# An issue edge in the feed-forward part: the low half of a weight split moves behind a relu product

## The chip, the cores and the metric

The kernel runs on one core of one Trainium2 chip. The metric is the device time of one execution in microseconds (us). TensorE is PE in the rows (PEld its weight loads), VectorE is DVE, ScalarE is ACT, GpSimd is POOL, and SP is the engine that issues most transfers.

## The reference

One layer of a decoder block on a sequence of 1024 with width 1024. The change touches only its last two lines, the feed-forward part.

```
h = h + mixed @ w_out
hidden = jnp.square(jax.nn.relu(rmsnorm(h, norm2_gain) @ w_ff_in))   # 1024 x 4096
return h + hidden @ w_ff_out
```

## The kernel before

The feed-forward part works on one eighth of the 4096 hidden channels at a time: 8 pairs, each of an "up" phase (a piece of `w_ff_in`) and a "down" phase (a piece of `w_ff_out`), 16 phases in all. Each phase multiplies 2x2 blocks by Strassen's scheme in seven products, P1, P5, P6, P2, P7, P3, P4 in an up phase and P1, P5, P6, P3, P7, P2, P4 in a down phase. I call each product a step. Each product is made of float32r matmuls of a high and a low part: `hi*hi + hi*lo + lo*hi`, so that a step is 24 matmuls of 128x512 (`group`). In a row the tile that is named last is the one in the weights' place (`whi`, `wlo`) and the other one is streamed.

Around each step the other engines make operands for steps to come:

- `split_w` makes a step's weights: ACT casts the block to `whi`, DVE subtracts to get `wlo` (L936, L937). It is called one step ahead, under a raised priority. `whi` and `wlo` have two buffers each.
- After an up step the block of hidden values is finished in place: DVE adds the PSUM result (L1069), `act2` multiplies the relu with the norm's factors `r2` on DVE (L1001), and ACT squares (L1004). For P4 the relu reads PSUM directly (L1065) and so frees the PSUM bank `y0`. The blocks are c11 (from P2), c22 (P7), c12 (P3) and c21 (P4). In most rows their numbers are left out, so that all are `c`.
- `rhs` makes a down step's right-hand side: for P5, P6, P7 and P4 a difference of two blocks on DVE (`less`, L1021), then a cast to `thi` on ACT (L1031) and a subtraction to `tlo` on DVE (L1032). P5 of the down phase takes c12 - c11, P6 takes c22 - (c12 - c11), P7 takes c22 - c12.
- After each half of a down step DVE adds the PSUM result to `h` (L1094).
- POOL makes sums and differences of weight blocks in place (L967, L968, L970 and others). In a down phase L968 overwrites the block that P1's `wlo` reads and L970 overwrites `wa`, which P5's `wlo` reads; each therefore waits for that subtraction.

A scheduler, led by priorities and by when it expects an operand, puts the instructions of each engine in one fixed order; each engine then runs its list in that order. The down phase's P1 and P6 go to the PSUM banks `x0`, `x1`, P5 and P3 to `y0`, `y1`, so that P5 of the down phase writes into the bank that P4 of the up phase filled.

Of the kernel before, what the change touches and what calls it, by code (L numbers as in the profile page):

```python
# [11 lines left out]
F32 = mybir.dt.float32  # L12
# [3 lines left out]
ALU = mybir.AluOpType  # L16
# [4 lines left out]
P = 128  # L21
# [3 lines left out]
HALF = 512  # L25
# [34 lines left out]
def hybrid_block(ctx, tc, x_ap, xt_ap, win_ap, lora_ap, wbr_ap, wout_ap, wff1_ap, wff2_ap, cst_ap,  # L60
                 vec_ap, eye_ap, amk_ap, out_ap, dbg=None):
    nc = tc.nc
    V, A, G, PE = nc.vector, nc.scalar, nc.gpsimd, nc.tensor
# [43 lines left out]
    def vs_(name):  # L107
# [10 lines left out]
                    op1=ALU.add)  # L118
# [29 lines left out]
    def w_tile(dt, tag):  # L148
        return wpool.tile([P, NK, 128], dt, tag=tag, name=tag, bufs=2)

    def load_w(src, nk=NK, eng=None):
        raw, hi, lo = w_tile(F32, "wraw"), w_tile(F32R, "whi"), w_tile(F32R, "wlo")
        for k in range(0, nk, 4):
            ks = slice(k, k + 4)
            nc.sync.dma_start(out=raw[:, ks], in_=src[:, ks])
            A.copy(out=hi[:, ks], in_=raw[:, ks])  # L156
            (eng or V).tensor_sub(out=lo[:, ks], in0=raw[:, ks], in1=hi[:, ks].bitcast(F32))  # L157
        return [(hi[:, k], lo[:, k]) for k in range(nk)]
# [622 lines left out]
    for ct in range(NK):  # L781
        w = load_w(wbr_ap[ct])
        for hf in range(2):
# [12 lines left out]
                                   op0=ALU.mult, op1=ALU.subtract)  # L796
# [10 lines left out]
    def fetch(ph, name, t):  # L807
        nc.sync.dma_start(out=t, in_=(wff1_ap, wff2_ap)[ph % 2][ph // 2, idx[name]])
        return t
# [60 lines left out]
    def norm2(op, pz):  # L870
        pk = pz[:, 0, 0:16].rearrange("p (a b) -> p a b", b=2)
        pkf = pk.rearrange("p a b -> p (a b)")
        for hf in range(2):
            head_sums(pkf, 8 * hf, hs[hf])
        sm = op.tile([P, 8], F32, tag="sm", name="sm")
        V.tensor_reduce(out=sm, in_=pk, axis=AX.X, op=ALU.add)
        return newton(op, sm, 8, 1.0 / D, RMS_EPS)
# [17 lines left out]
    def res_sq(ct, hf):  # L895
        sl = slice(hf * HALF, (hf + 1) * HALF)
        if ct == 0:
            A.activation(out=hs[hf], in_=h[ct][:, sl], func=AF.Square)
        else:
            t = op.tile([P, HALF], F32, tag="tC", name="hq", bufs=2)  # L900
            A.activation(out=t, in_=h[ct][:, sl], func=AF.Square)
            V.tensor_add(out=hs[hf], in0=hs[hf], in1=t)

    def wout(ct):
        nc.sync.dma_start(out=h[ct], in_=xt_ap[ct * P:(ct + 1) * P, :])
        return load_w(wout_ap[ct])

    for ct in (0, 4, 1, 5, 2, 6):
        w = wout(ct)
# [11 lines left out]
    tags = (("m", 2), ("m", 2), ("s", 2), ("s", 2))  # L921
    pss = [(pm if t == "m" else pp).tile([P, HALF], F32, tag=t, name="ps_o", bufs=n) for t, n in tags]
    for k in range(NK):
        for j in range(4):
            w, sl = ws_[j // 2][k], slice((j % 2) * HALF, (j % 2 + 1) * HALF)
# [4 lines left out]
    gst = ExitStack()  # L930
    hp = gst.enter_context(tc.tile_pool(name="hpool", bufs=1, side="right"))

    def split_w(src, pool=None, tags=("whi", "wlo")):
        hi, lo = (w_tile(F32R, t) if pool is None else pool.tile([P, NK, 128], F32R, tag=t, name=t) for t in tags)
        with tc.high_priority(offset=HP_F):
            A.copy(out=hi, in_=src)  # L936
            V.tensor_sub(out=lo, in0=src, in1=hi.bitcast(F32))  # L937
        return hi, lo

    w0 = split_w(raw["a11"], hp, ("c21", "c22"))  # L940
    s1 = hp.tile([P, NK, 128], F32, tag="c12", name="s1")
    V.tensor_add(out=s1, in0=raw["a21"], in1=raw["a22"])  # L942
# [9 lines left out]
    r2 = mpool.tile([P, T], F32, tag="m14", name="r2")  # L952
    wa = mpool.tile([P, NK, 128], F32, tag="m15", name="wa")
    lo_, hi_ = slice(0, HALF), slice(HALF, T)
    hp2 = None
    nxt = {}

    def weight(ph, name):
        def ahead(new, old):
            if ph < 15:  # L960
                nxt[new] = fetch(ph + 1, new, raw[old])

        a11, a21, a12, a22 = (raw[k] for k in ("a11", "a21", "a12", "a22"))
        sm = wa if ph else s1
        w = w0 if ph == 0 and name == "P1" else split_w({"P1": a11, "P5": sm, "P6": a11, "P2": a12, "P7": a21, "P3": wa, "P4": a22}[name])
        if name == ("P5", "P1")[ph % 2]:
            G.tensor_sub(out=a21, in0=a11, in1=a21)  # L967
            G.tensor_sub(out=a11, in0=sm, in1=a11)  # L968
        elif name == "P6":
            (G if ph else V).tensor_sub(out=wa, in0=a12, in1=a11)  # L970
            ahead("a21", "a11")
        elif ph % 2 == 0:
            if name == "P2":
                ahead("a22", "a12")
            elif name == "P7":
                ahead("a11", "a21")
            elif name == "P3":
                G.tensor_add(out=wa, in0=nxt["a21"], in1=nxt["a22"])
            elif name == "P4":
                ahead("a12", "a22")  # L980
        else:
            if name == "P7":
                ahead("a11", "a21")
            elif name == "P2":
                ahead("a12", "a12")
            elif name == "P4":
                ahead("a22", "a22")
                if ph < 15:
                    G.tensor_add(out=wa, in0=nxt["a21"], in1=nxt["a22"])
        return w  # L990
# [6 lines left out]
                n += 1  # L997

    def act2(c, hf):
        if hf is not None:  # L1000
            V.scalar_tensor_tensor(out=c, in0=c, scalar=0.0,  # L1001
                                   in1=r2[:, (lo_, hi_)[hf]].unsqueeze(1).broadcast_to([P, 2, HALF]),
                                   op0=ALU.max, op1=ALU.mult)
        A.activation(out=c, in_=c, func=AF.Square)  # L1004

    rhs1 = {"P1": "B11", "P5": "T1", "P6": "T2", "P2": "B21", "P7": "T3", "P3": "B22", "P4": "T4"}
    dst1 = {"P1": "c11", "P5": "c22", "P6": "c12", "P2": "c11", "P7": "c22", "P3": "c12", "P4": "c21"}
# [5 lines left out]
    def bank(tag):  # L1013
        return (pf if tag[0] == "y" else px).tile([P, 2, HALF], F32, tag=tag, name="ps" + tag)
# [4 lines left out]
    def rhs(name):  # L1019
        def less(out, a):  # L1020
            V.tensor_sub(out=C[out], in0=C[a], in1=C[out])  # L1021

        if name == "P7":
            less("c12", "c22")
        with tc.high_priority(offset=HP_F if name in ("P5", "P6") else 0):
            if name in ("P5", "P6", "P4"):
                less("c11", {"P5": "c12", "P6": "c22", "P4": "c21"}[name])
            src = C[{"P3": "c22", "P7": "c12", "P2": "c21"}.get(name, "c11")]
            hi = hp2.tile([P, 2, HALF], F32R, tag="thi", name="thi", bufs=2)
            lo = hp2.tile([P, 2, HALF], F32R, tag="tlo", name="tlo", bufs=2)  # L1030
            A.copy(out=hi, in_=src)  # L1031
            V.tensor_sub(out=lo, in0=src, in1=hi.bitcast(F32))  # L1032
        R[name] = (hi, lo)

    def up(n, name, w):
        if name == "P1":
            for b in ("y0", "y1", "x0")[:2 if n == 0 else 3]:
                Z[b] = bank(b)
        if n == 0:
            if name not in ("P1", "P5"):  # L1040
                next(more, None)
            if name == "P6":
                for ct in (3, 7):
                    for hf in range(2):
                        res_sq(ct, hf)
                Z["rs"] = norm2(op, px1)
            if name == "P4":
                rhs("P1")
                rhs("P5")
        ps = Z[{"P5": "y1", "P3": "y1", "P2": "x0"}.get(name, "y0")]  # L1050
        hi, lo = w
        for a in range(2):
            group(ps[:, a], [((hi[:, 4 * a + k], lo[:, 4 * a + k]), B[rhs1[name]][k]) for k in range(4)],
                  name in ("P1", "P5", "P2"))
        cn = dst1[name]
        if name in ("P1", "P5", "P6", "P4"):
            C[cn] = hp.tile([P, 2, HALF], F32, tag=cn, name=cn)
        c = C[cn]
        if n == 0 and name == "P2":
            for hf in range(2):  # L1060
                spread(hf, Z["rs"], px1)
        if name in ("P1", "P5", "P6"):
            A.copy(out=c, in_=ps)
        elif name == "P4":
            V.scalar_tensor_tensor(out=c, in0=ps, scalar=0.0, in1=r2[:, lo_].unsqueeze(1).broadcast_to([P, 2, HALF]),  # L1065
                                   op0=ALU.max, op1=ALU.mult)
            act2(c, None)
        else:
            V.tensor_add(out=c, in0=c, in1=ps)  # L1069
            act2(c, 0 if name == "P2" else 1)  # L1070
            if hp2 is not None and name != "P7":
                rhs({"P2": "P1", "P3": "P5"}[name])

# [24 lines left out]

    steps = [(ph, name) for ph in range(16) for name in order[ph % 2]]
    w = weight(0, "P1")  # L1100
    for g, (ph, name) in enumerate(steps):
        nw = None
        if g + 1 < len(steps):
            if steps[g + 1][1] == "P1":
                raw, nxt = nxt, {}
# [6 lines left out]
        w = nw  # L1112
# [98 lines left out]
```

## Time and profile before

| what | before |
|---|---|
| median of 3 runs | 1527.97 us (1526.92 to 1528.69) |
| profiled execution | 1529.62 us, its span 1527.8 us |
| PE busy | 1491.3 us, 98% of the span |
| DVE busy | 1044.1 us, 68% |
| ACT busy | 639.1 us, 42% |
| POOL busy | 192.2 us, 13% |

The span runs from the first to the last recorded instruction. A busy share is an average over stages that differ: the feed-forward matmuls begin at 882 us of the span and go on to its end, and within each pair the load of DVE swings from nearly idle to unbroken.

### The profile page before, as it was taken

How to read it: one execution, taken by the hardware profiler on the slowest of the kernel's cores; microseconds unless marked ns; L12 is line 12 of the kernel's file. 1: busy time of each engine (PE TensorE's matmuls, PEld its weight loads, DVE VectorE, ACT ScalarE, POOL GpSimd, SP SyncE). 2: the span in 40 equal slices, each digit the busy share in tenths (PEclk: the TensorE clock that was granted, in tenths of full speed). 3: DMA queues.
4: the chain of work that ended last, by engine and by line, in shares of the span. 5: the costliest groups of instructions: out<-in, count | busy, mean ns of one | idle time of the engine just before them, and what ended most of it. 6: DMA issues, size and time to landing. Idle time of an engine off the chain costs nothing.

```text
span 1527.8 us, 22206 instructions
## 1 busy us (share of the span) xinstructions
PE 1491.3 (98%) x8396; PEld 1177.2 (77%) x8396; DVE 1044.1 (68%) x2056; ACT 639.1 (42%) x1126; POOL 192.2 (13%) x116
## 2 busy tenths in 40 slices
PE   5999999999999999999999999999999999999998
PEld 5878777777777777788888787878787878787776
DVE  4232678888988875353656579595858687776867
ACT  6332436456545665441224354332424333423332
POOL 1000000000000000000000111323223232323230
PEclk9999999999999999999999999999999999999999
DMA  5455334334222323383433111111120111111112
GB/s 192 165 149 146 109 103 149 103 104 120 88 90 66 103 84 124 117 295 113 136 125 146 42 42 56 56 42 69 42 69 28 69 42 65 46 56 42 56 55 111
DMA packets 99771, 145.65 MB, mean 95 GB/s; under 512 B 26448, under 2 KB 48848, under 8 KB 99664
## 3 DMA queue, kind: packets, MB, share of 16 engines
q1 hardware_dynamic: 99664, 144.23, 28.8%
q8 instruction: 66, 1.08, 0.3%
q14 instruction: 41, 0.34, 0.1%
HBM read 108.54 MB, written 35.65 MB: 94 GB/s over the span
## 4 chain that ended last, share of the span: by engine, by line
PE 75%; DVE 19%; ACT 3%; issue 2%; DMA 1%; SPq 0%; DVEq 0%; ACTq 0%
PE ps_m L164 32%; PE psy L996 15%; PE psx L996 12%; DVE wlo L937 4%; DVE c L1021 2%; DVE c L1001 2%; DVE tlo L1032 2%; PE po L164 2%; PE ps_o L927 1%; PE pu L170 1%; DVE h L1094 1%; ACT c L1004 1%; ACT whi L936 1%; PE pk L246 1%; PE ps_s L170 1%
## 5 line engine op out<-in xcount | busy, mean ns | idle before, releaser
L164 PE MATMUL ps_m<-uh,wlo 128*128 128x512 f32 x576 | 235.5, 409 | 0.0
L164 PE MATMUL ps_m<-ul,whi 128*128 128x512 f32 x576 | 234.3, 407 | 0.0
L164 PE MATMUL ps_m<-uh,whi 128*128 128x512 f32 x576 | 233.0, 404 | 0.0
L996 PE MATMUL psy<-T,whi 128*128 128x512 f32 x512 | 159.6, 393 | 0.0
L164 PEld LDWEIGHTS ps_m<-uh,whi 128*128 128x128 f32 x576 | 108.6, 189 | 21.2 <-issue 0.8
L164 PEld LDWEIGHTS ps_m<-uh,wlo 128*128 128x128 f32 x576 | 108.6, 189 | 21.1 <-issue 0.6
L164 PEld LDWEIGHTS ps_m<-ul,whi 128*128 128x128 f32 x576 | 108.7, 189 | 20.2 <-issue 0.7
L996 PEld LDWEIGHTS psy<-T,whi 128*128 128x128 f32 x512 | 96.1, 188 | 21.9
L157 DVE TENSOR_TENSOR wlo<-wraw,whi 128x512 fp32r<-128x512 f32 x101 | 67.9, 687 | 56.6 <-ACT whi L156 56.4
L996 PE MATMUL psx<-tlo,whi 128*128 128x512 f32 x256 | 101.9, 398 | 4.5 <-DVE tlo L1032 4.5
L937 DVE TENSOR_TENSOR wlo<-fraw_a,whi 128x1024 fp32r<-128x1024 f32 x47 | 66.0, 1405 | 57.5 <-ACT whi L936 57.5
L936 ACT CAST whi<-fraw_a 128x1024 fp32r<-128x1024 f32 x47 | 49.3, 1049 | 129.1 <-PE psy L996 85.7
L996 PE MATMUL psx<-thi,wlo 128*128 128x512 f32 x256 | 101.6, 398 | 1.5 <-DVE h L1094 0.9
L996 PE MATMUL psx<-thi,whi 128*128 128x512 f32 x256 | 101.0, 395 | 0.0
L996 PE MATMUL psy<-T,wlo 128*128 128x512 f32 x256 | 100.6, 393 | 0.0
L967 POOL TENSOR_TENSOR fraw_a<-fraw_a,fraw_a 128x1024 f32<-128x1024 f32 x16 | 45.5, 2846 | 346.7 <-DVE s L942 345.5
L1094 DVE TENSOR_TENSOR h<-h,psx 128x1024 f32<-128x1024 f32 (+1 forms) x66 | 76.8, 1179 | 9.6 <-PE psx L996 9.6
L996 PE MATMUL psy<-tlo,whi 128*128 128x512 f32 x192 | 77.2, 402 | 3.1 <-DVE tlo L1032 3.1
L156 ACT CAST whi<-wraw 128x512 fp32r<-128x512 f32 x105 | 61.0, 619 | 45.4 <-PE ps_m L164 45.3
L996 PE MATMUL psy<-thi,wlo 128*128 128x512 f32 x192 | 75.8, 395 | 0.0
L996 PE MATMUL psy<-thi,whi 128*128 128x512 f32 x192 | 75.8, 395 | 0.0
L996 PE MATMUL psy<-B,whi 128*128 128x512 f32 x240 | 74.8, 393 | 0.0
(298 smaller groups left out, 3227.1 us busy)
## 6 DMA issues: line engine op xcount, KB each, us to landing
wraw<-win SPq DMA_DIRECT2D x72, 256.0 KB, 3.3
fraw_a<-wff SPq DMA_DIRECT2D x32, 512.0 KB, 3.2
wraw<-wff SPq DMA_DIRECT2D x32, 512.0 KB, 3.2
gate_d<-gt SPq DMA_DIRECT2D x32, 256.0 KB, 2.0
z_d<-zt SPq DMA_DIRECT2D x24, 256.0 KB, 2.3
xt<-x SPq DMA_DIRECT2D x8, 512.0 KB, 5.7
la<-wa_d SPq DMA_DIRECT2D x8, 512.0 KB, 4.3
aq<-q_d SPq DMA_DIRECT2D x8, 512.0 KB, 4.2
```

The source lines that it names most:

```text
L156: A.copy(out=hi[:, ks], in_=raw[:, ks])
L157: (eng or V).tensor_sub(out=lo[:, ks], in0=raw[:, ks], in1=hi[:, ks].bitcast(F32))
L164: PE.matmul(out=out, lhsT=a, rhs=b, start=(n == 0), stop=(n == last))
L170: after = PE.matmul(out=out, lhsT=lhsT, rhs=rhs, start=start, stop=stop).ins
L936: A.copy(out=hi, in_=src)
L937: V.tensor_sub(out=lo, in0=src, in1=hi.bitcast(F32))
L967: G.tensor_sub(out=a21, in0=a11, in1=a21)
L996: PE.matmul(out=out, lhsT=a, rhs=b, start=start and n == 0, stop=n == last, skip_group_check=True)
L1001: V.scalar_tensor_tensor(out=c, in0=c, scalar=0.0, in1=r2[:, (lo_, hi_)[hf]].unsqueeze(1).broadcast_to([P, 2, HALF]), op0=ALU.max, op1=ALU ...
L1021: V.tensor_sub(out=C[out], in0=C[a], in1=C[out])
L1032: V.tensor_sub(out=lo, in0=src, in1=hi.bitcast(F32))
L1094: V.tensor_add(out=ht, in0=ht, in1=ps[:, c0 % 2:c0 % 2 + step])
```

## The change

The relu product of c12 (made in up step P3) is remembered, and the subtraction that makes `wlo` for P1 of the following down phase gets an issue edge on DVE: it stands behind that relu in DVE's list. An issue edge orders two instructions in one engine's list; it adds no wait. The number of instructions is the same on each engine, and PE's order is the same.

```diff
-    def split_w(src, pool=None, tags=("whi", "wlo")):
+    def split_w(src, pool=None, tags=("whi", "wlo"), after=None):
...
             A.copy(out=hi, in_=src)
-            V.tensor_sub(out=lo, in0=src, in1=hi.bitcast(F32))
+            with tc.issue_after(after) if after is not None else nullcontext():
+                V.tensor_sub(out=lo, in0=src, in1=hi.bitcast(F32))
...
+        w = w0 if ph == 0 and name == "P1" else split_w({"P1": a11, "P5": sm, "P6": a11, "P2": a12, "P7": a21, "P3": wa, "P4": a22}[name],
+                                                       after=relu.get((ph, name)))
...
-            act2(c, 0 if name == "P2" else 1)
+            last = act2(c, 0 if name == "P2" else 1)
+            if name == "P3":
+                relu[2 * n + 1, "P1"] = last
```

The scheduler then lays out DVE's list anew around the edge. This is DVE in the second pair before, from the addition for c12 to the addition of P1's second half to `h` (`wlo_10083` is P1's, `wlo_10116` and `tlo_10079` are P5's, all of the down phase):

```order
L1069 TENSOR_TENSOR c12_9975<-c12_9975,psy1_9886 128x1024
L937 TENSOR_TENSOR wlo_10083<-fraw_a21_8902,whi_10082 128x1024
L1001 SCALAR_TENSOR_TENSOR c12_9975<-c12_9975,r2_9323 128x1024
L1021 TENSOR_TENSOR c11_9912<-c12_9975,c11_9912 128x1024
L1065 SCALAR_TENSOR_TENSOR c21_10112<-psy0_9885,r2_9323 128x1024
L937 TENSOR_TENSOR wlo_10116<-wa_9324,whi_10115 128x1024
L1032 TENSOR_TENSOR tlo_10079<-c11_9912,thi_10078 128x1024
L1094 TENSOR_TENSOR h_8664<-h_8664,psx0_10119 128x2x512
L1021 TENSOR_TENSOR c11_9912<-c22_9944,c11_9912 128x1024
L1094 TENSOR_TENSOR h_8664<-h_8664,psx1_10120 128x2x512
```

And this is the same place of DVE's list in the changed kernel:

```order
L1073 TENSOR_TENSOR c12_9975<-c12_9975,psy1_9886 128x1024
L1004 SCALAR_TENSOR_TENSOR c12_9975<-c12_9975,r2_9323 128x1024
L938 TENSOR_TENSOR wlo_10083<-fraw_a21_8902,whi_10082 128x1024
L1025 TENSOR_TENSOR c11_9912<-c12_9975,c11_9912 128x1024
L1025 TENSOR_TENSOR c12_9975<-c22_9944,c12_9975 128x1024
L1036 TENSOR_TENSOR tlo_10079<-c11_9912,thi_10078 128x1024
L938 TENSOR_TENSOR wlo_10116<-wa_9324,whi_10115 128x1024
L1025 TENSOR_TENSOR c11_9912<-c22_9944,c11_9912 128x1024
L1069 SCALAR_TENSOR_TENSOR c21_10112<-psy0_9885,r2_9323 128x1024
L1100 TENSOR_TENSOR h_8664<-h_8664,psx0_10119 128x2x512
L1100 TENSOR_TENSOR h_8664<-h_8664,psx1_10120 128x2x512
```

Besides the swap of `wlo` and c12's relu, the difference for P7 (c12 - stored into c12) came up from behind P6's operands, the difference for P6 stands ahead of the additions to `h`, and the relu of c21 went from fifth place to ninth, behind all three differences and P5's two subtractions.

On ACT two casts changed places in each pair. Before, at the same place (`whi_10115` and `thi_10078` are P5's):

```order
L1004 ACTIVATE c12_9975<-c12_9975 128x1024
L936 CAST whi_10115<-wa_9324 128x1024
L1031 CAST thi_10078<-c11_9912 128x1024
L1004 ACTIVATE c21_10112<-c21_10112 128x1024
L936 CAST whi_10147<-fraw_a21_8902 128x1024
```

In the changed kernel:

```order
L1007 ACTIVATE c12_9975<-c12_9975 128x1024
L1035 CAST thi_10078<-c11_9912 128x1024
L936 CAST whi_10115<-wa_9324 128x1024
L1007 ACTIVATE c21_10112<-c21_10112 128x1024
L936 CAST whi_10147<-fraw_a21_8902 128x1024
```

P5's streamed operand now comes ahead of P5's weights. The rest of ACT's list is unmoved. All 8 pairs change alike.

## Rows read from the trace of the kernel before

**Rows 1.** The page: busy time by engine, and the granted clock in 40 slices.

```profile
PE 1491.3 (98%) x8396; PEld 1177.2 (77%) x8396; DVE 1044.1 (68%) x2056; ACT 639.1 (42%) x1126; POOL 192.2 (13%) x116
...
PEclk9999999999999999999999999999999999999999
```

**Rows 2.** The chain of waits, second pair: start us, length us, what.

```profile
1026.91 5.57 PE psx L996 x24
```

**Rows 3.** The timeline of PE, second pair: start us, length us, instruction, [idle before].

```profile
1008.04 0.40 PE L996 MATMUL psy<-thi,wlo 128*128 128x512 f32 x1
1008.88 0.50 PE L996 MATMUL psy<-tlo,whi 128*128 128x512 f32 x1 [0.44 <-DVE tlo L1032]
1009.21 0.39 PE L996 MATMUL psy<-thi,whi 128*128 128x512 f32 x1
...
1014.58 0.47 PE L996 MATMUL psx<-thi,wlo 128*128 128x512 f32 x1
1015.63 0.50 PE L996 MATMUL psx<-tlo,whi 128*128 128x512 f32 x1 [0.58 <-DVE tlo L1032]
...
1021.31 0.48 PE L996 MATMUL psy<-tlo,whi 128*128 128x512 f32 x1
1021.63 0.39 PE L996 MATMUL psy<-thi,whi 128*128 128x512 f32 x1
```

**Rows 4.** Who waited for the tile tlo, whole kernel: us in total, times.

```profile
  PE psx L996: 4.5, 8
  PE psy L996: 3.1, 7
```

**Rows 5.** The timeline of DVE, second pair.

```profile
997.57 1.21 DVE L1069 TENSOR_TENSOR c<-c,psy 128x1024 f32<-128x1024 f32 x1
999.70 1.23 DVE L937 TENSOR_TENSOR wlo<-fraw_a,whi 128x1024 fp32r<-128x1024 f32 x1 [0.93 <-ACT whi L936]
1000.85 1.22 DVE L1001 SCALAR_TENSOR_TENSOR c<-c,r 128x1024 f32<-128x1024 f32 x1
1003.19 2.23 DVE L1021 TENSOR_TENSOR c<-c,c 128x1024 f32<-128x1024 f32 x1 [1.13 <-ACT c L1004]
1005.34 1.22 DVE L1065 SCALAR_TENSOR_TENSOR c<-psy,r 128x1024 f32<-128x1024 f32 x1
1006.48 1.21 DVE L937 TENSOR_TENSOR wlo<-wa,whi 128x1024 fp32r<-128x1024 f32 x1
1007.61 1.22 DVE L1032 TENSOR_TENSOR tlo<-c,thi 128x1024 fp32r<-128x1024 f32 x1
1008.74 1.21 DVE L1094 TENSOR_TENSOR h<-h,psx 128x1024 f32<-128x1024 f32 x1
1009.88 2.30 DVE L1021 TENSOR_TENSOR c<-c,c 128x1024 f32<-128x1024 f32 x1
```

**Rows 6.** The timeline of ACT, second pair.

```profile
1002.10 1.06 ACT L1004 ACTIVATE c<-c 128x1024 f32<-128x1024 f32 x1 [2.43 <-DVE c L1001]
1003.06 1.03 ACT L936 CAST whi<-wa 128x1024 fp32r<-128x1024 f32 x1
1005.46 1.05 ACT L1031 CAST thi<-c 128x1024 fp32r<-128x1024 f32 x1 [1.36 <-DVE c L1021]
```

**Rows 7.** The timeline of POOL, second pair and the beginning of the third.

```profile
1001.08 3.26 POOL L968 TENSOR_TENSOR fraw_a<-wa,fraw_a 128x1024 f32<-128x1024 f32 x1 [6.79 <-DVE wlo L937]
1007.82 3.27 POOL L970 TENSOR_TENSOR wa<-wraw,fraw_a 128x1024 f32<-128x1024 f32 x1 [3.48 <-issue]
...
1044.10 2.40 POOL L968 TENSOR_TENSOR fraw_a<-wa,fraw_a 128x1024 f32<-128x1024 f32 x1
```

**Rows 8.** The timeline of DVE, first pair.

```profile
918.38 1.22 DVE L1069 TENSOR_TENSOR c<-c,psy 128x1024 f32<-128x1024 f32 x1 [0.56 <-PE psy L996]
```

**Rows 9.** The timeline of PE, first pair.

```profile
929.32 0.40 PE L996 MATMUL psy<-thi,wlo 128*128 128x512 f32 x1
...
935.82 0.51 PE L996 MATMUL psx<-tlo,whi 128*128 128x512 f32 x1 [0.52 <-DVE tlo L1032]
```

**Rows 10.** Busy time of each engine in a stretch: us, PE, PEld, DVE, ACT, POOL, PEclk, DMA, GB/s.

```profile
1518.00:1527.80 9.80, 4.86 (x20) 3.12 (x18) 2.81 (x5) 0.00 (x0) 0.00 (x0) 0.95 0.45 170
```

More of the change, by code (lines that the diff above doesn't have):

```diff
@@ L955, in hybrid_block @@
     hp2 = None
-    nxt = {}
+    nxt, relu = {}, {}
     def weight(ph, name):
@@ L964, in weight @@
         sm = wa if ph else s1
-        w = w0 if ph == 0 and name == "P1" else split_w({"P1": a11, "P5": sm, "P6": a11, "P2": a12, "P7": a21, "P3": wa, "P4": a22}[name])
+        w = w0 if ph == 0 and name == "P1" else split_w({"P1": a11, "P5": sm, "P6": a11, "P2": a12, "P7": a21, "P3": wa, "P4": a22}[name],
+                                                       after=relu.get((ph, name)))
         if name == ("P5", "P1")[ph % 2]:
@@ L999, in act2 @@
     def act2(c, hf):
+        last = None
         if hf is not None:
-            V.scalar_tensor_tensor(out=c, in0=c, scalar=0.0,
-                                   in1=r2[:, (lo_, hi_)[hf]].unsqueeze(1).broadcast_to([P, 2, HALF]),
-                                   op0=ALU.max, op1=ALU.mult)
+            last = V.scalar_tensor_tensor(out=c, in0=c, scalar=0.0,
+                                          in1=r2[:, (lo_, hi_)[hf]].unsqueeze(1).broadcast_to([P, 2, HALF]),
+                                          op0=ALU.max, op1=ALU.mult).ins
         A.activation(out=c, in_=c, func=AF.Square)
+        return last
     rhs1 = {"P1": "B11", "P5": "T1", "P6": "T2", "P2": "B21", "P7": "T3", "P3": "B22", "P4": "T4"}
```

## The prediction, made before the changed kernel was run

> **What bounds the kernel now.** I read the page first: PE is busy for 98% of the span, and the granted clock stands at 9 tenths or more in every slice, which is the 2.4 GHz level [rows 1]. So a change can win only where PE waits, and there is little of that. The chain of waits gives the pace of an undisturbed step: 24 matmuls in 5.57 us, 0.232 us from one to the next [rows 2].
>
> Then I looked for the places in a pair where PE falls behind this pace. In the second pair there are three [rows 3]. P5 of the down phase: its first matmul starts at 1008.04, the second only at 1008.88, and the third 0.33 behind that. So 0.84 - 0.23 = 0.61 is lost in the wait and 0.10 in the restart. P6: 22 matmuls at pace after 1009.21 would bring its first to 1014.31, it starts at 1014.58 (0.27 lost); the second comes 1.05 later (0.82 lost), and I count 0.10 for the restart as before. P3 loses 0.09 (0.32 from second to third). Together **1.99 us per pair**. All the large waits are for DVE's `tlo`, in P5 (PSUM bank y) 7 times and in P6 (bank x) 8 times [rows 4]: so seven pairs show both, and the first pair shows only the one in P6.
>
> Why is `tlo` late? In DVE's rows [rows 5] the c12 addition starts at 997.57. Then DVE waits 0.93 for a cast of ACT before it can make P1's `wlo`, and c12's relu stands behind this. ACT's square is therefore late (1002.10 to 1003.16, [rows 6]), and DVE waits 1.13 for it. The two differences then take 2.23 and 2.30 us, where their seven like-sized neighbours take 1.21 to 1.23 [rows 5]. Rows of POOL lie over both: L968 from 1001.08 to 1004.34, L970 from 1007.82 to 1011.09 [rows 7]. The first difference ends 1.08 behind L968's end and the second 1.09 behind L970's: each stood until POOL's instruction was over. The other direction holds too. POOL's 3.26 is 0.86 more than the 2.40 of the same line alone [rows 7]; it started while c12's relu was running and got going about 0.13 before the relu's recorded end. The addition to `h` at 1008.74, which reads PSUM, took its normal 1.21 under L970 [rows 5, 7].
>
> **The change part by part, in the second pair.** No instruction is added or removed, and PE's order is the same; what counts is when DVE finishes what P5 needs.
>
> *What it gains.* The addition for c12 ends at 998.78. The relu needs its result, so I start it there: 998.80 to 1000.02, where before it started at 1000.85 [rows 5]. ACT's square follows 0.03 behind, as before: 1000.05 to 1001.11 [rows 6]. P1's `wlo` fills DVE meanwhile: neighbours start 1.13 apart [rows 5], so 999.94 to 1001.16. That is 0.24 later than before (999.70), and it costs nothing: P1's first matmul comes 24 matmuls before 1008.04, at 1002.47. So P5's difference can start at 1001.14, 2.05 earlier than the 1003.19 of before.
>
> *What it loses to POOL.* L968 starts 0.15 behind the end of P1's `wlo`, as before (999.70 + 1.23 = 1000.93, then 1001.08 [rows 5, 7]): at 1001.31, when P5's difference has just started. Before, L968 ended 3.49 behind the start of the instruction that held it up (1000.85 to 1004.34); so now at 1001.14 + 3.49 = 1004.63. The next in DVE's list is the difference for P7, which overwrites the c12 that P5's difference reads. It has to see that one finished at 1002.36, and by then POOL, which took over 0.13 before the recorded end of the relu, has begun. The difference stands and ends 1.08 behind POOL: 1005.71. Here the trace shows no case in which POOL waits while DVE has two such instructions in a row. The bounds are nothing (DVE keeps going, the difference ends at 1003.61) and the 2.1 us of this paragraph. I take the upper one, by the row of L968.
>
> The Trainium skill, page "SBUF — State Buffer", section "SBUF: two separate sides", says that GpSimd and a VectorE instruction with two SBUF inputs share a port pair that is locked for a whole instruction, so that the loser stands fully. By that rule this term is all of POOL's rest, about the 2.1 us of the rows; by an even sharing of the ports both would only be slowed, POOL's work would lie beside DVE's, and the sum would come near that of the first rival below. The two long differences agree with the lock, and this rule speaks against the change.
>
> *The rest of the list.* ACT's cast to `thi` for P5 and then the one for its weights run from 1002.4 to 1004.5 (1.05 and 1.03, [rows 6]), under POOL's instruction. DVE goes on at its spacing of 1.13: `tlo` for P5 1005.63, `wlo` for P5 1006.76, P6's difference 1007.89, c21's relu 1009.02 to 1010.24. L970 starts when P5's `wlo` is done (1007.97 + 0.13) and is held up by P6's difference; the relu behind that reads PSUM like the addition at 1008.74 and isn't held up by POOL.
>
> *What is queued behind it.* P5's first matmul writes bank `y0`, which c21's relu has to empty. Before, that relu was done at 1006.56, ahead of everything that P5 needs. Now it comes last, and PE waits for it: with 0.06 to LDWEIGHTS and 0.03 to the matmul (1007.61 + 1.22 = 1008.83 to 1008.88 was the same hand-over), P5 starts at 1010.33 instead of 1008.04. With the restart that is 2.29 + 0.10 = **2.39 lost**. P6 no longer waits: behind the relu come two additions to `h`, then P6's `wlo` and `tlo`, which is done at 1009.02 + 4 x 1.13 + 1.22 = 1014.8, and P6's second matmul is due at 1016.2. P3's `tlo` follows P5's second addition, two subtractions later, 1.5 us ahead of PE, so its 0.09 goes too.
>
> *The sum.* Seven pairs: 2.39 - 1.99 = +0.40 each, 2.8 us. First pair: there the addition starts at 918.38, 79.19 before that of the second pair [rows 5, 8], so P5 can start at 1010.33 - 79.19 = 931.14, while its first matmul now starts at 929.32 [rows 9]: 1.82 + 0.10 lost. Before, 25 matmuls at pace would have brought P6's second to 935.12; it came at 935.82 [rows 9], so 0.70 + 0.10 was lost there, and 0.09 in P3. That is +1.03. In all +3.8, **about +4 us**: 1533.6 against the profiled execution's 1529.62, whose span is 1527.8. The median of the runs shown is 1527.97, 1.65 lower, so I expect **1532.0**. An error of 0.15 in when the relu ends is 1.2 us in the sum.
>
> **The rivals.** A measurement of this kernel tells a change from none at about 0.2%, 3.1 us.
>
> *First, faster.* DVE keeps the ports from instruction to instruction, and POOL gets them only when the PSUM-reading relu comes. Then DVE's list runs on: P7's difference to 1003.61, `tlo` 1003.53, `wlo` 1004.66, P6's difference 1005.79, c21's relu 1006.92 to 1008.14. P5 starts at 1008.23, 0.29 lost with the restart; P6 perhaps 0.1, since L970 now falls on its `wlo`. Seven pairs gain 1.6 and the first 0.8: 12 us, 1516. It decides where c21's relu ends before 1009.84, 0.4 earlier than I work out. For it: no row shows that queue. Against it: the rows in which POOL takes over ahead of the recorded end, and the wait of P7's difference, which opens a gap.
>
> *Second, POOL goes first.* If P5's difference is 0.17 later than I reckon, L968 (1001.31) takes the ports ahead of it and ends at 1003.71; the difference ends at 1004.80, P7's at about 1006.0, and all behind is 0.3 later: +2.4, 1534.4.
>
> *Third, no difference.* The edge moves the same two microseconds from P6's `tlo` to P5's bank, and small errors of mine (hand-overs, the restart) make up the 0.4 per pair: 1528 to 1531.
>
> *Fourth, the clock.* PE would stand for over 2 us at one place, more than the 1.05 between two matmuls of before. The granted clock fell below 1.00 only at the end, 0.95 in the last 9.8 us, with PE busy for half of it [rows 10]. If it fell to its 1.2 GHz level for one step after each stall, 24 matmuls would take 5.57 us more, 45 us in all, 1573. The Trainium skill, page "TensorE: Matmul & The Clock Gate", section "Why this matters for your kernels", warns of idle gaps between bursts of matmuls for this reason; the stalls of before did not show it.
>
> **How the numbers follow.** My forecast (P5 waits for c21's relu, the sum between +2 and +6) has 0.70. The first rival has 0.10, the second 0.07, the third 0.11, the fourth 0.02. Slower by over 0.2% is most of the forecast (0.57 of it, since +4 is only 1 us above the bound), the second and the fourth: 0.66. Within 0.2%: the rest of the forecast and the third, 0.24. Faster: 0.10. The range 1527.5 to 1535.5 takes in the third rival and the second, and leaves out the first, the fourth and about 0.06 of tails. The forecast's own range is 1530 to 1534.
>
> **What would show it.** In the changed kernel: c12's relu directly behind its addition; P5's difference at the normal 1.2; P7's at over 3 us with POOL's L970 (the old L968) over it; c21's relu as the last of nine, ended 12.6 to 12.8 behind the addition's start; PE waiting in seven or eight pairs at P5's *first* matmul for about 2.3 us with DVE's c21 named, and no longer at P6. It is wrong if P7's difference takes 1.2 (the first rival), if P5's takes 2.2 (the second), or if P6 still waits for `tlo`.

## The result and the profile after

The changed kernel takes 1544.05 us (1541.91 to 1544.71, 4 runs) against 1527.63 us of the kernel before: a ratio of 1.0104, 95% interval 1.0091 to 1.0117. I forecast +4 us, and it is +16. The direction and the chain of waits were right; a cost that I had as a rival at 0.02 came on top.

First DVE of the changed kernel in the second pair, which answers to [rows 5]. The rows are merged where one line runs twice in succession; the last row shows the second of the two merged differences by itself.

```profile
998.46 1.21 DVE L1073 TENSOR_TENSOR c<-c,psy 128x1024 f32<-128x1024 f32 x1
999.71 1.23 DVE L1004 SCALAR_TENSOR_TENSOR c<-c,r 128x1024 f32<-128x1024 f32 x1
1000.85 1.22 DVE L938 TENSOR_TENSOR wlo<-fraw_a,whi 128x1024 fp32r<-128x1024 f32 x1
1002.06 4.58 DVE L1025 TENSOR_TENSOR c<-c,c 128x1024 f32<-128x1024 f32 x2
1006.56 1.21 DVE L1036 TENSOR_TENSOR tlo<-c,thi 128x1024 fp32r<-128x1024 f32 x1
1007.70 1.21 DVE L938 TENSOR_TENSOR wlo<-wa,whi 128x1024 fp32r<-128x1024 f32 x1
1008.83 1.21 DVE L1025 TENSOR_TENSOR c<-c,c 128x1024 f32<-128x1024 f32 x1
1009.97 1.21 DVE L1069 SCALAR_TENSOR_TENSOR c<-psy,r 128x1024 f32<-128x1024 f32 x1
...
1003.32 3.31 DVE L1025 TENSOR_TENSOR c<-c,c 128x1024 f32<-128x1024 f32 x1
```

The relu of c12 stands directly behind its addition, the differences for P5 and P7 take 4.58 together, of which P7's takes 3.31, and the relu of c21 ends at 1011.18, last of its group. POOL in the same stretch, beside [rows 7]:

```profile
1002.21 3.34 POOL L970 TENSOR_TENSOR fraw_a<-wa,fraw_a 128x1024 f32<-128x1024 f32 x1 [7.02 <-DVE wlo L938]
1009.04 3.23 POOL L972 TENSOR_TENSOR wa<-wraw,fraw_a 128x1024 f32<-128x1024 f32 x1 [3.49 <-issue]
```

L970 starts 0.15 behind the start of P5's difference, and P7's difference ends 1.09 behind L970's end (1006.64 and 1005.55). Now PE at P5, beside [rows 3]:

```profile
1008.71 0.40 PE L998 MATMUL psx<-thi,whi 128*128 128x512 f32 x1
1011.32 0.66 PE L998 MATMUL psy<-thi,wlo 128*128 128x512 f32 x1 [2.22 <-DVE c L1069]
1011.78 0.63 PE L998 MATMUL psy<-tlo,whi 128*128 128x512 f32 x1
1012.21 0.63 PE L998 MATMUL psy<-thi,whi 128*128 128x512 f32 x1
...
1014.34 0.63 PE L998 MATMUL psy<-tlo,whi 128*128 128x512 f32 x1
1014.77 0.44 PE L998 MATMUL psy<-thi,whi 128*128 128x512 f32 x1
1015.05 0.39 PE L998 MATMUL psy<-thi,wlo 128*128 128x512 f32 x1
1015.28 0.39 PE L998 MATMUL psy<-tlo,whi 128*128 128x512 f32 x1
```

PE stands (has nothing to run) for 2.22 us and waits for `c L1069`, the relu of c21. What my sum left out comes behind it: matmuls start 0.43 apart instead of 0.23 and take 0.63, for about nine matmuls, and then the old pace is back at once. The granted clock says why. Stretches of the second pair, columns as in [rows 10]:

```profile
1009.00:1011.30 2.30, 0.11 (x1) 0.01 (x1) 2.30 (x3) 0.09 (x1) 2.26 (x1) 1.00 0.00 0
1011.30:1014.80 3.50, 3.48 (x9) 2.76 (x10) 3.50 (x4) 2.86 (x3) 0.97 (x1) 0.52 0.00 0
1014.80:1018.00 3.20, 3.20 (x15) 2.63 (x14) 2.13 (x2) 0.00 (x0) 0.00 (x0) 0.99 0.50 169
```

While PE stands the clock is still at 1.00; in the 3.5 us after that it is at 0.52, the 1.2 GHz level but for an edge, and then it is back at 2.4 GHz. From 1011.32 to 1015.05 nine intervals take 3.73 us, at pace they would take 2.09: 1.64 us are lost, the restart included. The same is to be read in all 8 pairs, with 9 or 10 stretched intervals and 1.63 or 1.64 us each. The fall does not come at one fixed moment of the restart. In the last pair three matmuls run at 1.00 before it:

```profile
1502.35:1502.95 0.60, 0.60 (x3) 0.51 (x4) 0.60 (x1) 0.60 (x1) 0.60 (x1) 1.00 0.00 0
1503.00:1506.00 3.00, 3.00 (x9) 2.32 (x8) 3.00 (x4) 2.19 (x3) 0.30 (x1) 0.50 0.01 3
```

P6 no longer waits. Its second matmul, which stood for `tlo` before, follows the first at the old pace:

```profile
1018.54 0.39 PE L998 MATMUL psx<-thi,wlo 128*128 128x512 f32 x1
1018.77 0.39 PE L998 MATMUL psx<-tlo,whi 128*128 128x512 f32 x1
```

### The profile page after: what moved, and what is told of

Read it like the earlier page. It is cut to its first block, busy times and chain, and to the rows that moved or that the text cites. A ratio compares the mean times of both kernels' runs of the same rounds, so it can differ in the third digit from the quotient of the medians.

```text
span 1542.8 us, 22198 instructions
## 1 busy us (share of the span) xinstructions
PE 1498.5 (97%) x8396; PEld 1187.6 (77%) x8396; DVE 1047.6 (68%) x2056; ACT 637.1 (41%) x1126; POOL 192.4 (12%) x116
## 3 DMA queue, kind: packets, MB, share of 16 engines
q8 instruction: 66, 1.08, 0.3%
## 4 chain that ended last, share of the span: by engine, by line
PE 79%; DVE 17%; issue 2%; ACT 1%; DMA 1%; SPq 0%; DVEq 0%; ACTq 0%
PE ps_m L164 32%; PE psy L998 19%; PE psx L998 12%; DVE c L1025 3%; DVE wlo L938 3%; PE po L164 2%; PE ps_o L927 1%; PE pu L170 1%; DVE c L1073 1%; DVE tlo L1036 1%; DVE c L1004 1%; PE pk L246 1%; PE ps_s L170 1%; PE ry L644 1%; PE pd L654 1%
## 5 line engine op out<-in xcount | busy, mean ns | idle before, releaser
L998 PE MATMUL psy<-thi,wlo 128*128 128x512 f32 x192 | 81.3, 423 | 17.3 <-DVE c L1069 17.3
L998 PE MATMUL psy<-thi,whi 128*128 128x512 f32 x192 | 80.9, 421 | 0.0
L998 PE MATMUL psy<-tlo,whi 128*128 128x512 f32 x192 | 80.8, 421 | 0.0
L1007 ACT ACTIVATE c<-c 128x1024 f32<-128x1024 f32 x32 | 34.0, 1061 | 107.7 <-DVE c L1004 60.5
```

Source lines behind the costliest of these rows:

```text
L998: PE.matmul(out=out, lhsT=a, rhs=b, start=start and n == 0, stop=n == last, skip_group_check=True)
```

## The experiments

All but fill2 and no_a11 ran on the same chip, beside 14 runs of the kernel before with a median of 1528.65 us. The theories are: A, the clock fell because PE stood still; B, P5's matmuls are slow because of their operands or their neighbours; C, the time lies elsewhere in the new order; D, for one run, a difference that follows another is long of itself.

**fill9, fill4 and fill2: keep the wait, but not the standing still.** The changed kernel with matmuls that nobody needs, ahead of P5 of each down phase. They write a bank that P5 overwrites. This is fill9; fill4 has 4 in place of 9, and fill2 has 2.

```diff
-    nxt, relu = {}, {}
+    nxt, relu, F = {}, {}, {}
...
+        if name == "P5":
+            for _ in range(9):
+                PE.matmul(out=Z["y1"][:, 0], lhsT=F["w"], rhs=F["t"], start=True, stop=True, skip_group_check=True)
+        F["w"], F["t"] = hi[:, 0], th[:, 0]
```

> The changed kernel with 9 extra matmuls of 128x512 on TensorE ahead of P5 of each down phase, into the bank y1 that P5 overwrites anyway (the output is unchanged). They take about 9 x 0.232 = 2.1 us of the 2.6 us in which TensorE stands there for the relu of c21, so the wait itself stays. Theory A (the clock fell because TensorE stood still; the excess over my +4 is the price of the half clock): the granted clock is back at 1.00, P5 again takes 0.232 per matmul, and the time is about 1527.6 + 4 = 1531 to 1533. Theory B (P5's matmuls are slow because of their operands or because of what VectorE and GpSimd do beside them): still 1543 to 1545. Theory C (the extra time lies elsewhere in the changed order): also 1543 to 1545.

Measured: 1534.34 us, ratio 1.0035 (1.0023 to 1.0048), granted clock 0.999 over the span.

> As fill9, but with 4 extra matmuls, about 0.9 us, so that TensorE still stands for about 1.4 us behind them. Theory A: between the two: if a stand of 1.4 us is short enough, as the two of 0.8 and 1.0 before were, 1531 to 1533; if it is too long, about 1544. Theories B and C: 1543 to 1545.

Measured: 1532.65 us, ratio 1.0025 (1.0015 to 1.0035), granted clock 1.00. PE of fill4 at P5 in the second pair (L1095 are the extra matmuls):

```profile
1007.72 1.10 PE L1095 MATMUL psy<-thi,whi 128*128 128x512 f32 x4
1010.10 0.47 PE L998 MATMUL psy<-thi,wlo 128*128 128x512 f32 x1 [1.28 <-DVE c L1069]
1010.41 0.39 PE L998 MATMUL psy<-tlo,whi 128*128 128x512 f32 x1
1010.64 0.40 PE L998 MATMUL psy<-thi,whi 128*128 128x512 f32 x1
```

The wait for c21's relu is the same, P5 still starts 2.6 us behind P1's last matmul; PE stands for 1.28 us of it, and behind it the pace is 0.23. Theory A holds, and B and C, which wanted 1543 to 1545, fall. The scheduler moved one instruction of DVE besides: P4's difference stands four places earlier, behind P5's first addition to `h`, in all three fill kernels. P5 waits as before, so this does not bear on the pace behind the wait. Fill9 lies 1 to 2 us above fill4; its intervals overlap with fill4's, and I did not follow it up.

> As fill4, with 2 extra matmuls, about 0.5 us, so that TensorE stands for about 1.9 us ahead of P5, between the 1.4 that left the clock at 1.00 and the 2.4 that didn't. If the clock is lost somewhere between, the time is either near 1532.5, with the granted clock 1.00, or near 1544, with 0.99; a value between would say that the clock falls in some of the pairs or for fewer matmuls.

Measured, beside 9 runs of the kernel before with a median of 1528.13 us: 1534.02 us, ratio 1.0039 (1.0027 to 1.0052), granted clock 1.00.

```profile
1009.29 0.63 PE L1095 MATMUL psy<-thi,whi 128*128 128x512 f32 x2
1011.70 0.47 PE L998 MATMUL psy<-thi,wlo 128*128 128x512 f32 x1 [1.77 <-DVE c L1069]
1012.00 0.39 PE L998 MATMUL psy<-tlo,whi 128*128 128x512 f32 x1
```

Even a stand of 1.77 us leaves the clock alone here, in the second pair and alike in the six behind it. But in the first pair of the changed kernel PE stands 1.77 us too, and there the clock falls.

```profile
927.20 0.40 PE L998 MATMUL psx<-thi,whi 128*128 128x512 f32 x1
929.37 0.64 PE L998 MATMUL psy<-thi,wlo 128*128 128x512 f32 x1 [1.77 <-DVE c L1069]
929.80 0.63 PE L998 MATMUL psy<-tlo,whi 128*128 128x512 f32 x1
```

So the length of the one stand alone doesn't decide; what else does stays open.

**relu21_ahead_of_p6: the relu of c21 one place earlier.** An issue edge puts P6's difference behind that relu.

```diff
         def less(out, a):
-            V.tensor_sub(out=C[out], in0=C[a], in1=C[out])
+            with tc.issue_after(relu["c21"]) if name in ('P6',) else nullcontext():
+                V.tensor_sub(out=C[out], in0=C[a], in1=C[out])
...
+            relu["c21"] = V.scalar_tensor_tensor(out=c, in0=ps, scalar=0.0,
...
```

> The changed kernel with one more issue edge on VectorE: P6's difference stands behind the relu of c21, which so moves up by one place in the list. Theory A: the relu ends 1.13 earlier, P5 loses 1.26 per pair with the restart instead of 2.39, and the clock may hold: 1527.6 - 7 x 0.73 = about 1522; if the clock falls all the same, about 1533. Theory B: about 1544 - 9 = 1535, since P5's matmuls stay slow. Theory C: within 3 us of 1544.

Measured: 1533.24 us, ratio 1.0028 (1.0016 to 1.004), granted clock 1.00. The clock held, but the time is 11 us above what theory A gave for that case: I had left something out. That it equals the 1533 worked out for a fallen clock is chance. PE in the third pair, at P5 and at P6:

```profile
1090.48 0.47 PE L998 MATMUL psy<-thi,wlo 128*128 128x512 f32 x1 [1.08 <-DVE c L1070]
...
1096.34 0.47 PE L998 MATMUL psx<-thi,wlo 128*128 128x512 f32 x1
1097.38 0.50 PE L998 MATMUL psx<-tlo,whi 128*128 128x512 f32 x1 [0.57 <-DVE tlo L1037]
```

P5's stand is down from 2.21 to 1.08, by the 1.13 worked out, but P6 waits again for its `tlo`, as in [rows 3]. DVE and POOL tell why:

```profile
1089.12 1.21 DVE L1070 SCALAR_TENSOR_TENSOR c<-psy,r 128x1024 f32<-128x1024 f32 x1
1090.26 2.54 DVE L1026 TENSOR_TENSOR c<-c,c 128x1024 f32<-128x1024 f32 x1
```

```profile
1089.33 2.38 POOL L972 TENSOR_TENSOR wa<-wraw,fraw_a 128x1024 f32<-128x1024 f32 x1 [3.49 <-issue]
```

With the relu between, P6's difference is no longer running when POOL's L972 comes; POOL has the ports first, and the difference takes 2.54 instead of 1.21. In the changed kernel it was the other way round: the difference at 1008.83 was ahead of L972 at 1009.04. So both of POOL's instructions now lie in the path, one ahead of P5 and one ahead of P6. P5 and P6 together lose about 2.4 us per pair, more than the 1.99 of the kernel before, and over the 8 pairs this makes up the 4.3 us measured.

**relu21_ahead_of_p6_p7: the relu under POOL's instruction.** As above, with `name in ('P6', 'P7')`, so that the relu of c21 comes directly behind P5's difference.

> As the one before, and P7's difference also stands behind the relu of c21, which so comes directly behind P5's difference, while GpSimd's instruction runs. Theory A: the relu reads PSUM and isn't held up, P5's and P6's operands are ready 0.5 us or more ahead of TensorE, no pair loses anything, the granted clock stays 1.00: 1527.6 - 7 x 1.99 - 0.9 = about 1513, faster than both kernels. Theory B: P5's matmuls stay slow in 8 pairs, about 1513 + 13 = 1526. Theory C: near 1544.

Measured: 1514.45 us (1513.89 to 1514.7), ratio 0.9906 (0.9893 to 0.992), granted clock 1.00: faster than both kernels, 14 us below the kernel before and close to the 1513 of theory A. DVE and POOL in the second pair:

```profile
998.94 1.23 DVE L1026 TENSOR_TENSOR c<-c,c 128x1024 f32<-128x1024 f32 x1
1000.42 1.23 DVE L1070 SCALAR_TENSOR_TENSOR c<-psy,r 128x1024 f32<-128x1024 f32 x1 [0.25 <-PE psy L998]
1001.56 1.96 DVE L1037 TENSOR_TENSOR tlo<-c,thi 128x1024 fp32r<-128x1024 f32 x1
1003.45 1.21 DVE L938 TENSOR_TENSOR wlo<-wa,whi 128x1024 fp32r<-128x1024 f32 x1
...
999.09 3.35 POOL L970 TENSOR_TENSOR fraw_a<-wa,fraw_a 128x1024 f32<-128x1024 f32 x1 [7.02 <-DVE wlo L938]
```

The relu, which reads PSUM, takes 1.23 in the time in which POOL holds the ports, and only 0.75 of POOL's instruction is left for `tlo` to wait out. The chain of waits is steps of PE alone:

```profile
1000.38 5.60 PE psx L998 x24
1005.98 5.60 PE psy L998 x24
1011.58 5.60 PE psx L998 x24
```

**no_a11: POOL's instruction left out.** The changed kernel without the subtraction of L970 in the down phases; the weights of P6 and what depends on them are therefore not the reference's.

```diff
-            G.tensor_sub(out=a11, in0=sm, in1=a11)
+            if ph % 2 == 0:
+                G.tensor_sub(out=a11, in0=sm, in1=a11)
```

> The changed kernel without GpSimd's subtraction for a11 in the down phases (the first of its two rows there), which is left out, so that the later weights of P6 and of the next blocks aren't the right ones; the order of VectorE around P5 stays. If P7's difference takes 3.4 us because GpSimd holds the ports (theory A), it takes 1.2 now, the relu of c21 ends 2.1 earlier, P5 loses about 0.3 per pair and the clock holds: about 1516. If a difference is long of itself there, because it follows another one (theory D): about 1544 as before.

Measured, beside the same runs of the kernel before as fill2: 1516.75 us (1515.94 to 1518.23), ratio 0.9925 (0.9912 to 0.9939), granted clock 0.999. The lists of the other engines are those of the changed kernel.

```profile
1000.97 2.48 DVE L1026 TENSOR_TENSOR c<-c,c 128x1024 f32<-128x1024 f32 x2
...
1007.61 0.40 PE L999 MATMUL psx<-thi,whi 128*128 128x512 f32 x1
1008.14 0.47 PE L999 MATMUL psy<-thi,wlo 128*128 128x512 f32 x1
```

The two differences take 2.48 together where they took 4.58, and of PE's wait at P5 0.30 is left (0.53 less 0.23), as worked out. Theory D falls: the 2.1 us were the wait for POOL.

## Why the prediction was wrong

**Right, with their sizes.** Measured from the addition for c12 in the second pair, the relu of c12 started at +1.25 (I had +1.23), P7's difference ended at +8.18 (+8.14) and the relu of c21 at +12.72 (+12.67). P5 lost 2.38 to the wait (2.29): the relu ended 0.05 later, and from its end to the matmul 0.14 passed, where I had put 0.09 beside a row that shows 0.05. P6 and P3 no longer waited. POOL took the ports between the two differences, which was the one bound that the rows before left open, and no_a11 shows that this is what the 2.1 us were. So the change saved the 2 us that I said, and handed P5 a wait of its own that was a little longer. The sum of these terms was +3.8, and with the standing still partly filled (fill4) it is measured at +0.25%, 3.8 us, with an interval from 2.3 to 5.3.

**Wrong: the pace behind the wait.** The step that failed is the term of the sum "2.29 + 0.10 = 2.39 lost" for P5. It priced what comes behind PE's wait as a restart of 0.10, with all further matmuls at the pace of [rows 2], and it did that because the waits of before in these pairs, up to 1.05 from one matmul to the next, had left the clock alone. I saw that the new wait was twice as long, and made that the fourth rival, with a chance of 0.02, so outside the range. It came true in all 8 pairs. Its size was also off: I priced it at one step, 24 matmuls and 5.57 us per pair; it was 9 or 10 intervals and 1.64 us per pair, 8 x 1.64 = 13.1 us. (That rival's total was wrong besides: 1573 is the time before and 45, without the +4 of the wait that it follows from; it should have been 1577.) Between the changed kernel and fill4, which have the same wait at P5, the ratios differ by 0.0079, 12 us. With the waits as measured, seven pairs lose 2.38 - 1.99 = 0.39 each; the first loses 1.94 (929.37 - 927.20, less 0.23) in place of 0.89, 1.05 more. That is again +3.8, and the restart is in the 1.64. So +3.8 + 13.1 = +16.9 stands against the +16.4 measured.

The Trainium skill, page "TensorE: Matmul & The Clock Gate", section "Why this matters for your kernels", names idle gaps between bursts of matmuls as what lowers the clock. The trace agrees in kind (0.52 granted behind stands of 2.22); how long a gap does it is for the rows to say, and here a stand of 1.77 was followed by a fall in one place and by none in another.

**The rivals.** The first (DVE keeps the ports) and the second (POOL goes ahead of P5's difference) did not occur: P5's difference ran first and P7's stood. The third, that the waits balance, comes near what is measured with the clock kept up (fill4, 0.25% above the kernel before); like my own sum it left out the clock.

## What to carry to other kernels

When instructions of one engine are put in another order, look for the one that empties a buffer that another engine has to fill next: here a relu that frees a PSUM bank was moved behind two differences that could wait, P6's and P7's, and this cost somewhat more than the edge had gained. A wait of TensorE is not priced by its length once it is longer than those that the trace has shown to be harmless: ask for the granted clock behind it, and if in doubt fill the head of the wait with matmuls that nobody needs. That gave back 12 us here (0.0079 of the time); putting the relu in a better place gave 30 (0.0198, from 1.0104 to 0.9906). Where GpSimd holds the shared ports, the work to put beside it is VectorE work that reads PSUM: here the relu took 1.23 us under GpSimd's instruction, and a difference of two SBUF blocks 3.31.

## What the runs showed of the hardware

In the changed kernel the clock fell behind the wait and not in it (1.00 granted in the 2.3 us in which PE stood, 0.52 in the 3.5 us after), in the last pair with three matmuls run at 1.00 between. It came back while PE worked at the lower level, after 1.63 or 1.64 us lost each time. Two, four or nine matmuls of 128x512 at the head of the wait were enough here to keep it up. A stand of 1.77 us was followed by a fall in the first pair of the changed kernel and by none in fill2; the runs don't say why. A VectorE subtraction of two SBUF blocks ended 1.08 or 1.09 us behind the end of GpSimd's instruction that had started first, and GpSimd got in between two such subtractions in a row, the second of which needs the first one's end.
